# Inverse blocks loaded through POOL's queue instead of SP's, their products six steps later

## The chip, the cores and the metric

The kernel runs on one core of a Trainium2 chip. The metric is the device time of one launch in microseconds (us); lower is better. Five engines work side by side, each through its own instructions in order: PE (matrix products), DVE and ACT (elementwise), POOL (elementwise, and it can issue DMA transfers), SP (issues DMA transfers only). An engine that waits at an instruction holds back everything behind it in its own queue.

## The reference

A two-layer decoder trunk over 512 positions of width 2048. Layer 0 is attention (a sparse group and a latent group). Layer 1, where the change lies, is RWKV-7: six mixed versions of the normed input are projected, and a 64x64 state per head (32 heads) is updated position by position.

```python
def step(state, inp):
    r_t, w_t, k_t, v_t, kk_t, a_t = inp
    sa = jnp.einsum('bhvk,bhk->bhv', state, -kk_t)
    state = (state * w_t[:, :, None, :] + sa[..., None] * (kk_t * a_t)[:, :, None, :]
             + v_t[..., None] * k_t[:, :, None, :])
    return state, jnp.einsum('bhvk,bhk->bhv', state, r_t)
...
xs = tuple(t.transpose(1, 0, 2, 3) for t in (r_h, w_h, k_h, v_h, kk, a_h))
_, y = lax.scan(step, s0, xs)
```

Then each head's output is normed, a bonus is added, a gate is applied, and one more projection leads to the residual and the final norm.

## The kernel before

Matrix products in float32 are done as three passes over split operands (`mm3`, L115 to L118: high by high, low by high, high by low), each of 128 rows by 512 columns. A weight tile of 512 KB (eight such blocks) is fetched by `wload` (L97): one DMA on SP's queue (L103) into one of two raw buffers, then a split by ACT (L85) and DVE (L86) into one of three pairs of split buffers. So PE can run only a few tiles ahead of the last weight that SP has fetched.

**The RWKV layer in chunks.** The 512 positions are cut into 8 chunks of 64, so that the scan becomes products of 64x64 blocks. That needs, for each chunk and head, the inverse of a triangular 64x64 matrix. The 32 heads are 16 pairs p, and four pairs make a group g (4 groups). For pair p, `pair` (L918) builds the operands; its last part (L986 to L994) makes the triangular blocks on PE (tile `pat`, L991), masks them on DVE (L993) and stores them to DRAM (`atd`, L994, on SP's queue).

**The inverses.** Behind the fourth pair of a group (p = 3, 7, 11, 15), three things are put into the program:

- `inverse` (L853): POOL loads the 32x32 diagonal blocks back from `atd` into `U` (four DMAs, L859) and inverts them in place by 30 steps of two small operations (L865, L867).
- `store` (L870): POOL transposes half of it into `T` (L872) and writes `U` and `T` to DRAM as `unu` (L873) and `unt` (L874).
- `inverse2` (L876), a generator of three parts. The first part loads eight blocks from DRAM, all on SP's queue: two from `unt` into `t11` (L884), two off-diagonal ones from `atd` into `t12` (L885) and four from `unu` into `u4` (L887). Here `t11`, `t12` and `u4` have one buffer each. The second part (L889 to L897) makes 64 products of 32x32 blocks of `t12` and `t11` on PE (tile `pv1`) and evicts them by ACT. The third (L899 to L907) makes 64 products with `u4` (tile `pu`), evicts them by DVE and stores the group's whole inverses (`utd`, L907, on SP's queue).

In the trace the tiles `t11` and `t12` have the name `inv2t`, `u4` has the name `u`, and `pv1` the name `pv`.

**What sets the order.** PE's order is written out by hand: `dense` (L1043) is one long stream of steps, a step being the three passes of one 128-row block; `fill(n)` (L1082) runs n steps, and `at(n, f)` (L1079) puts f into the program when n more steps have run. The five parts of `pair` p start around a step t0, which goes up by 18 for the first six pairs and by 22 for the rest; the triangular blocks come at t0 + 32. The three parts of `inverse2` come 70, 98 and 106 steps after the group's fourth pair (L1000). This stage of the kernel ends at step t0 + 32 + 108 of the last pair (L1098), and then the recurrence begins (L1102), which mixes its own small products with the rest of the stream (L1261 on). The other engines' queues are ordered by a scheduler that works from the program's order and its own cost estimates. All of SP's DMAs, weights among them, stand in one queue in that order.

## Time and profile before

| what | value |
|---|---|
| median of 3 runs | 2518.12 us (2512.82 to 2518.66) |
| profiled execution, its own time | 2516.01 us |
| profiled execution, span from first to last instruction | 2514.2 us |
| PE busy, of the span | 2257.8 us (90%) |
| DVE, ACT, POOL busy | 1604.8, 1020.3, 587.4 us |
| mean granted TensorE clock, of full speed | 0.957 |

The span is what the trace shows, from its first instruction to its last; the profiled execution's own time also holds the 1.8 us that lie around it. All stretches named below are in us from the span's start. The stage of the pairs and inverses, with the four groups, lies at about 1230 to 1775, and the recurrence at 1775 to 2320. Busy shares are averages over stages with different limits; what counts for an edit is which wait ends last in its own stage.

### The profile page before, as it was taken

The page shows a single profiled execution, that of the slowest core. Times are in us where ns is not written, and L with a number is a line of the kernel's source. Part 1 is how long each engine was busy: PE and PEld are TensorE (multiplying, and loading weights), DVE is VectorE, ACT ScalarE, POOL GpSimd, SP SyncE. Part 2 cuts the span into 40 slices and gives each one's busy share as a digit, 9 for nine tenths or more (in the row PEclk, how much of TensorE's full clock was granted, in tenths as well). Part 3 has the DMA queues.
Part 4 walks back from the last instruction along what each step waited for, and adds up shares of the span by engine and source line. Part 5 has one row for each costly group of instructions (what it writes and reads, how often), then busy time and mean ns, then how long its engine had stood idle before and what let it go on. Part 6 is the DMA issues. An engine that isn't in the chain of part 4 may idle for free. (4 is left out here: it accounts for less than half of the span.)

```text
span 2514.2 us, 38073 instructions
## 1 busy us (share of the span) xinstructions
PE 2257.8 (90%) x14148; PEld 1749.1 (70%) x14148; DVE 1604.8 (64%) x2983; ACT 1020.3 (41%) x1809; POOL 587.4 (23%) x823
## 2 busy tenths in 40 slices
PE   6789999999989989989995896886899999997997
PEld 3567777777767768866774774665677677775786
DVE  6973677778675557458565574661566666666755
ACT  3343344444454442233764665451133334444222
POOL 1100022222230101100025081643333333320111
PEclk9999999999999999999998897998999999999998
DMA  8973554444222268644674778774656654435864
GB/s 313 325 233 127 171 176 154 156 159 151 72 79 94 76 208 304 216 150 154 204 210 122 233 215 238 213 227 120 178 147 191 214 151 135 133 109 181 307 204 140
DMA packets 256124, 452.03 MB, mean 180 GB/s; under 512 B 104257, under 2 KB 118721, under 8 KB 254657
## 3 DMA queue, kind: packets, MB, share of 16 engines
q1 hardware_dynamic: 239426, 404.49, 50.1%
q0 software_dynamic: 14208, 43.01, 6.5%
q8 instruction: 111, 1.82, 0.3%
q10 hardware_dynamic: 2304, 2.10, 0.2%
q14 instruction: 75, 0.61, 0.1%
HBM read 365.88 MB, written 83.63 MB: 179 GB/s over the span
## 5 line engine op out<-in xcount | busy, mean ns | idle before, releaser
L86 DVE TENSOR_TENSOR wl<-raw,wh 128x1024 fp32r<-128x1024 f32 (+3 forms) x314 | 372.9, 1189 | 225.2 <-ACT wh L85 222.8
L85 ACT ACTIVATE wh<-raw 128x1024 fp32r<-128x1024 f32 (+3 forms) x314 | 313.4, 1000 | 491.7 <-PE pw L118 74.5
L199 DVE CUSTOM_DVE_ANT_0 adaw<-adaw,sc,mod 128x512 f32<-128x512 f32 (+1 forms) x160 | 158.8, 995 | 59.3 <-DMA adaw<-in_ada 57.1
L116 PE MATMUL ps_v<-xh,wh 128*128 128x512 f32 x256 | 109.8, 429 | 68.6 <-ACT wh L85 50.3
L199 DVE CUSTOM_DVE_ANT_0 adaw<-adaw,sc,vec 128x1024 f32<-128x1024 f32 (+1 forms) x96 | 121.1, 1262 | 45.5 <-DMA adaw<-in_ada 45.2
L116 PE MATMUL ps_r<-xh,wh 128*128 128x512 f32 x256 | 109.4, 427 | 19.9 <-ACT wh L85 18.5
L116 PE MATMUL pwo<-xho,wh 128*128 128x512 f32 (+1 forms) x288 | 109.7, 381 | 10.1 <-ACT xho L85 8.7
L470 POOL TENSOR_TENSOR pcmn<-csn,cmn 128x128 f32<-128x128 f32 x48 | 25.6, 560 | 394.3 <-ACT pn L291 206.6
L117 PE MATMUL pwo<-xho,wl 128*128 128x512 f32 (+1 forms) x288 | 108.6, 378 | 4.2 <-DVE wl L86 4.2
L116 PE MATMUL ps_z<-xh,wh 128*128 128x512 f32 x256 | 111.7, 436 | 0.0
L117 PE MATMUL ps_v<-xh,wl 128*128 128x512 f32 x256 | 106.5, 416 | 3.2 <-DVE wl L86 3.2
L118 PE MATMUL pwo<-xlo,wh 128*128 128x512 f32 (+1 forms) x288 | 109.3, 380 | 0.0
L116 PEld LDWEIGHTS ps_v<-xh,wh 128*128 128x128 f32 x256 | 51.3, 200 | 82.7 <-ACT wh L85 52.0
L118 PE MATMUL ps_v<-xl,wh 128*128 128x512 f32 x256 | 105.6, 412 | 0.1
L116 PE MATMUL pw<-yh,wh 128*128 128x512 f32 x256 | 101.5, 397 | 2.9 <-ACT yh L85 2.7
L118 PE MATMUL pw<-yl,wh 128*128 128x512 f32 x256 | 102.1, 403 | 2.0 <-DVE yl L86 2.0
L117 PE MATMUL ps_r<-xh,wl 128*128 128x512 f32 x256 | 102.8, 402 | 0.5 <-DVE wl L86 0.5
L118 PE MATMUL ps_r<-xl,wh 128*128 128x512 f32 x256 | 102.7, 401 | 0.4 <-DVE xl L745 0.4
L117 PE MATMUL pw<-yh,wl 128*128 128x512 f32 x256 | 101.4, 397 | 0.4 <-DVE wl L86 0.4
L118 PE MATMUL ps_z<-xl,wh 128*128 128x512 f32 x256 | 101.8, 397 | 0.0
L117 PE MATMUL ps_z<-xh,wl 128*128 128x512 f32 x256 | 101.6, 397 | 0.0
L499 POOL TENSOR_SCALAR pn<-pn,recn 128x128 f32<-128x128 f32 (+3 forms) x128 | 83.0, 666 | 32.6 <-DVE recn L495 31.1
(463 smaller groups left out, 6206.4 us busy)
## 6 DMA issues: line engine op xcount, KB each, us to landing
adaw<-in_ada SPq DMA_DIRECT2D x128, 512.0 KB, 6.9
adaw<-in_ada SPq DMA_DIRECT2D x128, 256.0 KB, 3.2
raw<-in_win_b SPq DMA_DIRECT2D x58, 512.0 KB, 3.7
raw<-in_rwo SPq DMA_DIRECT2D x36, 512.0 KB, 4.5
raw<-in_wout SPq DMA_DIRECT2D x32, 512.0 KB, 4.5
raw<-in_rwv SPq DMA_DIRECT2D x32, 512.0 KB, 5.4
raw<-in_rwr SPq DMA_DIRECT2D x32, 512.0 KB, 4.5
raw<-in_rwz SPq DMA_DIRECT2D x32, 512.0 KB, 3.9
```

The source lines that it names most:

```text
L85: nc.scalar.activation(hi, src, AF.Copy)
L86: nc.vector.tensor_tensor(lo, src, f32(hi), op=ALU.subtract)
L116: nc.tensor.matmul(ps, ah, bh, start=start, stop=False)
L117: nc.tensor.matmul(ps, al, bh, start=False, stop=False)
L118: nc.tensor.matmul(ps, ah, bl, start=False, stop=stop_)
L199: nc.vector.tensor_tensor_reduce(w, w, self.sc[:, i - self.i0:i - self.i0 + self.n], 0.5, v_("ada_b", layer * 48 + j) if i == 0 else m, op ...
L470: nc.gpsimd.tensor_tensor(pcm[:, :, r], cs, cm[:, 3][:, :, None].to_broadcast([P, 4, 32]), op=ALU.mult)
L499: nc.gpsimd.tensor_scalar(pb[i, b][:, :n], pb[i, b][:, :n], rec[:, i, b:b + 1], 1.0, op0=ALU.mult, op1=ALU.mult)
```

## The change

The eight loads of `inverse2` go from SP's queue to POOL's; the two parts on PE come 104 and 112 steps behind the group's fourth pair instead of 98 and 106; the stage's end is put six steps later to match. No arithmetic is changed, and no transfer is added or dropped.

```diff
             for h in range(2):
                 lo, hi = slice(64 * h, 64 * h + 32), slice(64 * h + 32, 64 * h + 64)
-                nc.sync.dma_start(t11[lo], tv[h])
-                nc.sync.dma_start(t12[lo], blocks(g, h, 0, 1))
+                nc.gpsimd.dma_start(t11[lo], tv[h])
+                nc.gpsimd.dma_start(t12[lo], blocks(g, h, 0, 1))
                 for b in range(2):
-                    nc.sync.dma_start(uu[(lo, hi)[b], :, 32 * b:32 * b + 32], uv[b, h])
+                    nc.gpsimd.dma_start(uu[(lo, hi)[b], :, 32 * b:32 * b + 32], uv[b, h])
...
                 inv = inverse2(p // 4)
-                for n in (70, 98, 106):
+                for n in (70, 104, 112):
                     at(n, lambda: next(inv, None))
...
-        while now[0] < t0 + 32 + 108:
+        while now[0] < t0 + 32 + 114:
             fill(1)
```

How the queues change can be read from the program's order of instructions. The first place is SP's queue around the loads of group 0 (a difference: rows with - stand only in the kernel before, rows with + only in the changed one; `raw` are weight tiles, `hin` inputs of the next version, `kpd` a scratch store):

```order
-L884 DMA inv2t11_0_12125<-unt_9906 32x32x32
+L103 DMA raw578_12190<-in_rwv 128x1024
 L767 DMA hin3_10_11959<-hd_9894 128x512
 L767 DMA hin3_11_11975<-hd_9894 128x512
 L916 DMA kpd_9902<-vf15_12052 128x512
-L887 DMA u4_10686<-unu_9905 32x32x32
+L103 DMA raw579_12254<-in_rwv 128x1024
 L767 DMA hin3_12_11988<-hd_9894 128x512
 L767 DMA hin3_13_12001<-hd_9894 128x512
```

Where the loads of `unt` and `unu` stood among the inputs of the next version, weight tiles stand now; the same holds at the other three groups.

The second place is POOL's queue between groups 0 and 1:

```order
 L873 DMA unu_9905<-U0_11496 128x1024
 L874 DMA unt_9906<-T0_11563 64x1024
+L887 DMA u4_10686<-unu_9905 32x32x32
+L884 DMA inv2t11_0_12125<-unt_9906 32x32x32
+L887 DMA u4_10686<-unu_9905 32x32x32
+L884 DMA inv2t11_0_12125<-unt_9906 32x32x32
+L887 DMA u4_10686<-unu_9905 32x32x32 x2
 L859 DMA U1_12748<-atd_9903 32x32x32 x4
+L885 DMA inv2t12_1_13470<-atd_9903 32x32x32
 L860 MEMSET U1_12748 128x32
 L865 TENSOR_TENSOR Ut1_12754<-U1_12748 128x30
+L885 DMA inv2t12_1_13470<-atd_9903 32x32x32
```

Six loads now follow the two stores, and the two of `t12` stand at the head of each group's inversion, one of them in front of its first operation.

The third place is PE at the first product of the inverses of group 0 (`pat6` are the triangular blocks of pair 6, `ps_v` the value projection):

```order
 L118 MATMUL ps_v1_2_12253<-xl3_15_12026,wh580_12336 128x512
-L991 MATMUL pat6_12461<-kk6_12093,bk6_12226 64x64 x16
+L991 MATMUL pat6_12391<-kk6_12093,bk6_12226 64x64 x16
+L895 MATMUL pv1_00_12411<-inv2t11_0_12125,inv2t12_0_12126 32x32 x32
+L895 MATMUL pv1_01_12446<-inv2t11_0_12125,inv2t12_0_12126 32x32 x32
 L116 MATMUL ps_v1_3_12484<-xh3_0_11765,wh581_12486 128x512
```

The products moved behind the end of one projection tile and behind the triangular blocks of pair 6; before, they stood six blocks earlier in the same tile.

## Rows read from the trace of the kernel before

**Rows 1.** Busy time by stretch: us, busy (count) by engine, PEclk, DMA share, GB/s.

```profile
1293.70:1774.60 480.90, 381.66 (x2871) 301.84 (x2870) 262.65 (x367) 230.07 (x361) 206.73 (x286) 0.89 0.68 198
1411.00:1499.00 88.00, 84.91 (x718) 68.26 (x716) 64.50 (x89) 61.95 (x104) 43.13 (x55) 1.00 0.78 242
1499.00:1550.00 51.00, 26.10 (x133) 20.07 (x135) 19.21 (x26) 17.79 (x30) 10.20 (x14) 0.70 0.63 174
```

**Rows 2.** PE's waits from 1293.7 to 1774.7: us in total, times, longest us.

```profile
PE ps_v L116 <- ACT wh L85: 50.3, 4, 23.8
PE ps_r L116 <- ACT wh L85: 18.5, 1, 18.5
PE ps_v L116 <- ACT xh L744: 18.2, 2, 17.7
```

**Rows 3.** SP's waits in the same stretch (same columns).

```profile
SPq L884 <- DMA unt<-T: 58.4, 4, 25.9
...
SPq L887 <- DMA unu<-U: 24.9, 1, 24.9
```

**Rows 4.** SP's timeline at group 0: start us, us, then engine, line, operation.

```profile
1337.12 0.32 SPq L916 DMA_DIRECT2D kpd<-vf  x1
1363.36 0.33 SPq L884 DMA_DIRECT2D inv2t<-unt  x1
```

**Rows 5.** PE's timeline, one row of each kind and the stage's ends (same columns).

```profile
1293.68 1.15 PE L991 MATMUL pat<-kk,bk 64*64 64x64 f32 x32
...
1338.44 0.40 PE L116 MATMUL ps_v<-xh,wh 128*128 128x512 f32 x1
...
1349.64 0.39 PE L116 MATMUL pl<-lh,l2hrw 96*128 96x512 f32 x1
...
1412.16 2.21 PE L895 MATMUL pv<-inv2t,inv2t 32*32 32x32 f32 x128
...
1418.70 1.15 PE L991 MATMUL pat<-kk,bk 64*64 64x64 f32 x32
...
1441.08 0.66 PE L1020 MATMUL pvt<-ca,vf 128*128 128x128 f32 x4
...
1478.29 1.15 PE L991 MATMUL pat<-kk,bk 64*64 64x64 f32 x32
...
1650.79 1.15 PE L991 MATMUL pat<-kk,bk 64*64 64x64 f32 x32
...
1774.65 0.46 PE L1141 MATMUL g<-kr,bk 64*128 64x128 f32 x2 [1.09 <-DMA kr<-krd]
```

**Rows 6.** POOL's timeline in groups 0 and 3 (same columns).

```profile
1309.20 0.16 POOL L860 MEMSET U<- 128x32 f32 x1 [4.17 <-DMA U<-atd]
...
1358.95 0.61 POOL L873 DMA_DIRECT2D unu<-U  x1
...
1669.95 0.15 POOL L860 MEMSET U<- 128x32 f32 x1 [8.07 <-DMA U<-atd]
...
1716.36 0.61 POOL L873 DMA_DIRECT2D unu<-U  x1
1716.96 0.56 POOL L874 DMA_DIRECT2D unt<-T  x1
```

**Rows 7.** Line 859, POOL's loads of U: issue in ns min/median/max, and landing.

```profile
L859 POOL DMA_DIRECT2D U<-atd x16: 783/786/1017, 1301.7 to 1661.1; - x16
...
DMA to landing us min/median/max: 4.1/5.4/8.7
```

**Rows 8.** Line 874, the store of unt: from issue to landing.

```profile
DMA to landing us min/median/max: 3.7/3.9/4.2
```

**Rows 9.** Line 884, the load from unt on SP's queue: from issue to landing.

```profile
DMA to landing us min/median/max: 2.4/3.7/5.9
```

**Rows 10.** The page's groups: DVE's split of a weight (busy, mean ns of one).

```profile
L86 DVE TENSOR_TENSOR wl<-raw,wh 128x1024 fp32r<-128x1024 f32 (+3 forms) x314 | 372.9, 1189 | 225.2 <-ACT wh L85 222.8
```

**Rows 11.** PE's timeline behind the recurrence.

```profile
2327.48 0.79 PE L116 MATMUL pwo<-xho,wh 128*128 128x512 f32 x1 [8.73 <-ACT xho L85]
```

## The prediction

> **What bounds the kernel now.** I read the busy time by stretch first, because shares over the whole span hide stages. From the triangular blocks of pair 3 (group 0) to the first product of the recurrence, 1293.68 to 1774.65 us [rows 5], the stage takes 481.0 us. PE is busy for 381.66 of 480.90 us there, so it idles 99.2 us, and the granted clock is 0.89 [rows 1]. Between groups it reads otherwise: from 1411 to 1499 PE is busy for 84.91 of 88 us at clock 1.00, from 1499 to 1550 for 26.10 of 51 us at 0.70 [rows 1]. The idle time comes in lumps.
>
> PE's waits say for what: 50.3 and 18.5 us for the split of a weight, 18.2 us for the inputs of the next version, single ones up to 23.8 us [rows 2]. Splits and inputs both start with a DMA on SP's queue, so I asked SP next. SP waits 58.4 us in four waits at L884 for the store of `unt`, and 24.9 us in one at L887 for `unu` [rows 3]: 83.3 us, once per group. The timeline shows the shape: SP issues a store at 1337.12 and nothing until the load of `unt` at 1363.36 [rows 4]. That store comes out of POOL's inversion, whose own store of `unu` leaves at 1358.95 [rows 6]. The weights stand behind the waiting load, and PE runs dry.
>
> **What the change moves.** Thirty-two DMAs (eight per group) leave SP. SP then never waits for POOL's inversion in front of a weight; what is left of it there is `utd`, which waits for PE's own products.
>
> *The stage without the lumps.* Between the two ends PE has 1366 passes of 512 columns, 13 sets of triangular blocks, 16 sets of transposes of `vf`, and four each of the products `pv` and `pu` (counted in its order). From 1338.44 to 1349.64 run 48 passes, 0.2333 us each [rows 5]. The others take 1.15, 0.66 and 2.21 us [rows 5] (`pu` taken as `pv`, its like). So 318.7 + 15.0 + 10.6 + 17.7 = 362.0 us. As a test, pair 6 to pair 9 comes to 60.0 us in this way, and the trace has 59.6 (1418.70 to 1478.29) [rows 5]. The stage's excess is 481.0 - 362.0 = 119.0 us: 99.2 idle, and some 20 of work at the lower of the two clock levels behind each idle time. All of it goes if nothing takes its place.
>
> *The six steps.* They bring 18 passes, 4.2 us, from the recurrence into this stage. The recurrence loses 4.2 us of filler. Behind it PE waits 8.73 us for its result [rows 11], so filler has little value at that end: bounds of the net cost 0 (all given back) and 4.2 us (nothing). I take 4.0, by that row.
>
> *POOL's own cost.* Nearest in shape are the 16 loads of `U`, 0.783 to 1.017 us per issue [rows 7]; I take 0.8. That is 6.4 us per group, beside POOL's other work: it idles more than half of the stage (206.73 of 480.90 us busy) [rows 1], so this costs nothing unless the products on PE come due first. SP in turn gets 32 issues off its queue; it does not bound the stage once it no longer waits, so I count nothing for that.
>
> *When the products come due.* This is what could take the place of the wait. Group 3 is tightest, because no pairs lie behind it: in PE's order, 104 steps (72.8 us), the triangular blocks (1.15), `pv` and `pu` of group 2 (4.4) and two sets of transposes (1.3), so `pv` is due 79.7 us after pair 15's blocks. POOL's side, from 1650.79 [rows 5]: the store of `unu` leaves at 1716.36, 65.6 us on, and that of `unt` 0.6 later [rows 6]. One load of `t12` now lies inside the inversion (0.8); the other is issued while POOL waits for `U` anyway (8.07 us) [rows 6]. So `unt` leaves at 67.0 and lands 3.9 us on [rows 8], at 70.9. Then come L884, L887, L884, the last issued at 72.5. A load lands 3.7 us after issue on SP's queue [rows 9] and 5.4 us for POOL's loads of `U`, 8.7 at worst [rows 7]: 76.2 to 81.2. I take 78, by POOL's own median, and so no wait; at worst 1.5 us. With the products still at 98 steps they would be due at 75.5, so the six steps are what buys the cover.
>
> Group 0 has 84.3 us (72.8, four sets of blocks 4.6, the operand products of three pairs 5.6, two sets of transposes 1.3) and the same path (store at 1358.95, 65.3 us after 1293.68 [rows 5, 6]). Groups 1 and 2 have about 92 us, since four pairs lie between.
>
> *A new wait on POOL.* The first load of `t12` of a group must wait until PE has read the one before. In groups 2 and 3 that product comes 12 to 15 us behind the group's triangular blocks, and POOL waits there with the inversion behind it. With the product (2.2) and the issue (0.8) the inversion is free at 15 to 18 us. In the trace it begins after 15.5 us in group 0 and 19.2 in group 3 (from pat to L860) [rows 5, 6]: group 2 may lose some 3 us of 12 spare ones, group 3 none.
>
> *What the feed can bear.* The stage moves 198 GB/s over 480.90 us; squeezed into about 370 us this is 257, against 242 at a DMA share of 0.78 in the stretch where PE never starved [rows 1]. That stretch idles 3.1 of 88 us, which over the stage would be 13; its idle end already belongs to the next block, so the bounds are 0 and 13, and I take 5.
>
> **The sum.** 2516.0 (the profiled execution's own time) - 119.0 + 5 + 4 + 1 (late products) = 2407 us. This execution lies 2.1 us under the median, so for the median I say 2408 us.
>
> **A page against the rows.** The Trainium skill, "SBUF — State Buffer", section "SBUF: two separate sides", speaks against this move: descriptors of a DMA issued from POOL are written by its own cores, and those are locked out while DVE runs certain copies; it gives 3100 ns instead of 620. By an estimate from that page eight issues per group would end some 20 us later, and the sum would be near 2455. The rows do not bear it out: of 16 issues from POOL the longest took 1.017 us [rows 7], beside a busy DVE.
>
> **The rivals.**
>
> *The products come late.* For it: group 3 has 2 us to spare by my reckoning, group 0 six, and POOL's loads will fly in a denser stage. Against it: the inversion ran in that time beside a fed PE already. If every issue waits for one DVE operation, 1.189 us [rows 10], the path grows by 9.5 us: PE waits 7 to 8 us in group 3 and 3 to 4 in group 0, and with the clock behind it 2408 + 13 = 2421. Twice that delay reaches all groups, some 2455. Chance 0.15; 0.03 of it for the lock at its worst.
>
> *The feed is next.* If transfers or the splits lag, PE idles 5 to 10% of 370 us instead of 5 us: 2421 to 2440. For it: 257 GB/s against 242. Against it: DVE, 64.50 of 88 us busy in the fed stretch [rows 1], has room. Chance 0.12.
>
> *Only issue time is saved.* If SP's wait hid behind something else that stops PE just as long (the inputs, DVE), the gain is SP's issues alone: 32 times 0.8, at most 26 us, and if none lies on PE's path nothing: 2490 to 2518. Against it: the lumps sit at SP's waits, 87 us of them on things that SP fetches [rows 2]. Chance 0.01. The Trainium skill, "DMA: Bandwidth & Descriptors", section "Issuing engines are not separate DMA queues", says as much: more issuing engines save only the time to initiate, usually small. By that rule the time would be the one just given; the rows disagree, since what stands in the queue is a wait and not an issue [rows 3, 4].
>
> *Slower.* POOL's queue now carries a loop: `pv` of one group must end before the next one's load of `t12`, the inversion stands behind that load, and the next `pv` behind the inversion. It decides once the inversion (1309.20 to 1358.95, 49.8 us with the copy [rows 6]) grows so long that the spare times are gone and PE waits more than the 119 us of now in four groups: 30 us each and about 8 to spare, so from 49.8 to 88 us. At twice the length PE would wait some 42 us per group, 168 in all, and at the lower clock behind it 2580. Nothing in the rows comes near; the two inversions shown take 49.8 and 46.4 us. Chance 0.02.
>
> **How the numbers follow.** The forecast has 0.70, the late products 0.15, the feed 0.12, issue time alone 0.01, slower 0.02. The range goes from 2396 (the whole excess gone, the filler free: 2516.0 - 119.0, rounded down) to 2440, which takes in the bounds of the feed (13), of the filler and of the landings, the feed rival and the milder late products; what is left out above and below is about 0.14. A measurement of this kernel tells 0.3% from no change. Faster by more than that: 0.70 + 0.15 + 0.12 = 0.97; within it 0.01; slower 0.02.
>
> **What would show it.** SP's waits at L884 and L887 are gone, and none takes their place beyond the few us at L907. PE is busy for about 97% of the stage at a clock near 1.00, and the stage takes some 370 us. `pv` shows no or a small wait for `inv2t`, in group 3 first. POOL's queue shows a wait before its first load of `t12` in group 2. Behind the recurrence PE waits some 12 us instead of 8.73. I am wrong if PE still has lumps of 10 us or more, wherever they wait, or if POOL's issues take over 1 us.

## The result, and the profile after

The changed kernel takes 2447.02 us (median of 4 runs, 2440.65 to 2447.81) against 2518.1 before in the same comparison: a ratio of 0.9717, 95% interval 0.9696 to 0.9738. Measured once more, with other kernels on another occasion, it took 2439.31 us (2432.07 to 2443.05), ratio 0.9694 (0.9671 to 0.9717). The forecast of 2408 us had the direction and the cause, but it was 39 us too low, and its range, which ended at 2440, stopped 7 us short. That the second measurement lies just inside the range is scatter between the two occasions and no merit of the forecast.

Busy time by stretch of the changed kernel, first the stage between the same two ends as in [rows 1], then two stretches inside it, from the triangular blocks of pair 7 to those of pair 8 and on to those of pair 12 (us, busy and count by engine, PEclk, DMA share, GB/s):

```profile
1297.24:1703.69 406.45, 381.52 (x2889) 303.34 (x2888) 268.60 (x367) 231.38 (x361) 250.34 (x323) 0.96 0.81 237
1414.80:1443.20 28.40, 22.12 (x115) 17.04 (x114) 18.01 (x28) 19.34 (x33) 12.93 (x20) 0.90 0.95 274
1443.20:1527.97 84.77, 80.05 (x574) 63.44 (x573) 60.82 (x80) 58.94 (x98) 55.39 (x70) 0.99 0.88 266
```

The stage went from 481.0 to 406.5 us, with PE idle for 24.9 us instead of 99.2 and a granted clock of 0.96 instead of 0.89. The stage gave 74.5 us back. Ahead of it this execution is 3.6 us longer (1297.24 against 1293.68) and behind it 2.6 (742.1 against 739.5). That makes the 68.4 us between the spans of 2514.2 and 2445.8. In the second measurement's profiled execution the stage is 407.0 us long and begins at 1288.38: the stage repeats well, and what lies ahead of it, where nothing was changed, scatters by some 9 us.

PE's waits from 1290 to 1700 us (total, times, longest), to be read against [rows 2]:

```profile
PE ps_v L116 <- ACT wh L85: 6.2, 2, 4.1
PE ps_v L117 <- DVE wl L86: 5.2, 3, 3.9
PE ps_v L116 <- ACT xh L744: 2.5, 1, 2.5
PE pu L904 <- ACT inv2v L897: 2.3, 1, 2.3
```

The lumps of up to 23.8 us are gone. What is left comes in pieces of some 4 us and less, and no product waits for `inv2t`. SP's waits from 1230 to 1720 us, to be read against [rows 3]:

```profile
SPq L103 <- DVE wl L86: 67.7, 38, 4.2
SPq L960 <- ACT em L959: 37.5, 14, 4.9
SPq L1034 <- DVE epr L1033: 29.0, 6, 11.8
SPq L980 <- DVE bk L979: 25.2, 15, 3.8
```

The 83.3 us at L884 and L887 are gone. The largest waits now are for free weight buffers (L103) and at the pairs' stores (L960, L980, L1034), 11.8 us at the longest. They are not new: in the kernel before, the four lines took 63.6, 34.5, 15.3 and 18.0 us (1230 to 1790). POOL's new lines, each from the view of one line (issue in ns min/median/max; its waits; landing), in the order L884, L885, L887:

```profile
L884 POOL DMA_DIRECT2D inv2t<-unt x8: 783/784/786, 1375.1 to 1671.2; - x8
...
DMA to landing us min/median/max: 4.4/7.5/9.1
...
L885 POOL DMA_DIRECT2D inv2t<-atd x8: 783/795/817, 1308.6 to 1615.9; - x8
...
  PE pv L895: 7.5, 2
...
L887 POOL DMA_DIRECT2D u<-unu x16: 783/783/854, 1372.9 to 1672.7; - x16
...
DMA to landing us min/median/max: 3.3/8.2/10.7
```

An issue costs POOL 0.78 to 0.85 us, as forecast from [rows 7]. But the loads of `unt` land 7.5 us after issue, where it was 3.7 on SP's queue [rows 9], in a stage that moved 198 GB/s instead of 237. The page shows the move as well: SP's queue (`q1`) carries 206146 packets instead of 239426, POOL's (`q0`) 15744 instead of 14208.

### The profile page after: what moved, and what is told of

Its sections match the earlier page's. It is cut to its first block, busy times and chain, and to the rows that moved or that the text cites. A ratio compares the mean times of both kernels' runs of the same rounds, so it can differ in the third digit from the quotient of the medians.

```text
span 2445.8 us, 38074 instructions
## 1 busy us (share of the span) xinstructions
PE 2258.9 (92%) x14148; PEld 1755.3 (72%) x14148; DVE 1609.8 (66%) x2983; ACT 1021.0 (42%) x1809; POOL 628.4 (26%) x855
## 3 DMA queue, kind: packets, MB, share of 16 engines
q1 hardware_dynamic: 206146, 400.30, 51.0%
q0 software_dynamic: 15744, 47.20, 7.6%
## 5 line engine op out<-in xcount | busy, mean ns | idle before, releaser
L116 PE MATMUL pwo<-xho,wh 128*128 128x512 f32 (+1 forms) x288 | 111.2, 386 | 10.7 <-ACT xho L85 7.7
L117 PE MATMUL ps_v<-xh,wl 128*128 128x512 f32 x256 | 104.0, 406 | 5.2 <-DVE wl L86 5.2
L867 POOL TENSOR_TENSOR U<-U,Ut 128x30 f32<-128x30 f32 (+14 forms) x120 | 96.1, 801 | 9.1
L865 POOL TENSOR_TENSOR Ut<-U 128x30 f32<-128x30 f32 (+14 forms) x120 | 91.2, 760 | 9.1
```

The lines of the kernel that those rows point to most:

```text
L116: nc.tensor.matmul(ps, ah, bh, start=start, stop=False)
L117: nc.tensor.matmul(ps, al, bh, start=False, stop=False)
L865: nc.gpsimd.tensor_tensor(tv, U[:, :s_, s_:s_ + 1].to_broadcast([P, s_, n]), U[:, s_:s_ + 1, s_ + 1:].to_broadcast([P, s_, n]), op=ALU.mult)
L867: nc.gpsimd.tensor_tensor(U[:, :s_, s_ + 1:], U[:, :s_, s_ + 1:], tv, op=ALU.add)
```

## Theories after the result

**Theory.** The loss of the kernel before was SP standing at loads whose data was not there yet. What the stage keeps over its priced work (406.5 against 362.0 + 4.2 = 366.2, so 40 us) is the supply of weights: transfers, and loads queued on SP behind stores. **Rivals.** The gain needs POOL's queue as such, or the six steps; the 40 us are ACT's and DVE's own order. Stage lengths below come from one profiled execution each, between the same two ends; the changed kernel gave 406.5 and 407.0 in two of them.

## Experiments: which part of the change did it

**Queue alone.** The loads on POOL, the products and the end where they were:

```diff
-                for n in (70, 104, 112):
+                for n in (70, 98, 106):
...
-        while now[0] < t0 + 32 + 114:
+        while now[0] < t0 + 32 + 108:
```

> The changed kernel with the products back at 98 and 106 steps (stage end at 108), the loads on POOL's queue. Theory (the loss was the wait at the head of SP's queue, and the queue alone removes it): 2440 to 2460 us, with at most a few us of PE waiting for inv2t in group 3, where the changed kernel had about 1 us to spare. Rival (the six steps do a large part): over 2470 us, with PE waits for inv2t of 10 us or more.

Measured: 2444.53 us, ratio 0.9702 (0.9675 to 0.9729). PE's wait for the loads in this kernel:

```profile
PE pv L895 <- DMA inv2t<-unt: 5.7, 2, 3.2
```

The queue alone brings all of the gain that can be measured. The later steps do what the forecast said (without them the products wait twice, 5.7 us), but buy no time that can be measured. The stage is 418.2 us against 406.5, yet the stretch behind it is 735.2 against 742.1.

**Steps alone.** The change with the loads left on SP:

```diff
-                nc.gpsimd.dma_start(t11[lo], tv[h])
-                nc.gpsimd.dma_start(t12[lo], blocks(g, h, 0, 1))
+                nc.sync.dma_start(t11[lo], tv[h])
+                nc.sync.dma_start(t12[lo], blocks(g, h, 0, 1))
...
-                    nc.gpsimd.dma_start(uu[(lo, hi)[b], :, 32 * b:32 * b + 32], uv[b, h])
+                    nc.sync.dma_start(uu[(lo, hi)[b], :, 32 * b:32 * b + 32], uv[b, h])
```

> The kernel before with the products at 104 and 112 steps (stage end at 114), the loads on SP's queue. Theory: SP still waits over 70 us at L884 and L887, and the time stays within 10 us of before, 2508 to 2528. Rival (the six steps do a large part): under 2490.

Measured: 2528.72 us, ratio 1.0053 (1.0036 to 1.0069), the stage 499.7 us. The time is 0.7 us above the theory's range, and SP waits 69.4 us at L884 and 25.4 at L887, a little more than before. By themselves the steps cost time.

**Loads later on SP.** As the run before, with the loads put into the program 98 steps behind the pair, not 70:

```diff
-                for n in (70, 104, 112):
+                for n in (98, 104, 112):
```

> As the last one, but the loads are put into the program 98 steps behind the group's fourth pair instead of 70, still on SP's queue. If the place in the program decides where they stand in SP's queue, the inversion is done by then and SP waits no more: 2435 to 2470. If the scheduler puts them as early as its own estimate allows, as the program's order suggests for group 0, SP's waits remain in part: 2480 to 2520. I expect the second.

Measured: 2559.43 us, ratio 1.0167 (1.0145 to 1.0188), slower than either case. PE's and SP's largest waits:

```profile
PE pv L895 <- DMA inv2t<-unt: 79.0, 3, 43.7
```

```profile
SPq L884 <- DMA unt<-T: 88.7, 3, 36.1
```

SP still reaches the loads before the inversion is done, and now the products stand directly behind them. So the later place in the program didn't help here.

**SP without the wait, first try.** The kernel before, its loads reading `atd` instead of `unu` and `unt` (so the inverses are left out), with `T` in the buffer of `v1` (otherwise `T` has the one buffer of `t11`, so that a load of `t11` would still wait for `T`'s store):

```diff
-            T = kw.tile([64, 32, 32], F32, tag="t11", name=f"T{g}", bufs=1)
+            T = kw.tile([64, 32, 32], F32, tag="v1", name=f"T{g}", bufs=1)
...
-                nc.sync.dma_start(t11[lo], tv[h])
+                nc.sync.dma_start(t11[lo], blocks(g, h, 0, 1))
...
-                    nc.sync.dma_start(uu[(lo, hi)[b], :, 32 * b:32 * b + 32], uv[b, h])
+                    nc.sync.dma_start(uu[(lo, hi)[b], :, 32 * b:32 * b + 32], blocks(g, h, b, b))
```

> The kernel before with the loads of t11 and u4 taken from atd instead of unt and unu, still on SP's queue, and T in the buffer of v1, so that no load waits for the inversion (this leaves out the inverses: the values are others). Theory (it is the wait, not the queue or the transfers): 2435 to 2460, as the changed kernel or a little better. Rival (what the change left, some 40 us of the stage over its work, is the loads' doing on POOL's queue, where they land in 8 us instead of 4): under 2430, and PE's waits in the stage fall by half against the changed kernel.

Measured: 2529.11 us, ratio 1.0054 (1.0037 to 1.0071). The shared buffer made a new wait: ACT's eviction into `v1` had to wait until `T` was stored (62.5 us in two waits), and PE's `pu` waited 92.5 us for it, 47.4 at once. The run says nothing on the queue.

**SP without the wait, second try.** The same reads, with `T`, its copy and its store left out:

```diff
-            T = kw.tile([64, 32, 32], F32, tag="t11", name=f"T{g}", bufs=1)
-            nc.gpsimd.tensor_copy(T, U[:64].rearrange("p s t -> p t s"))
...
-            nc.gpsimd.dma_start(unt[g], T.rearrange("p s t -> p (s t)"))
```

> The kernel before with all its loads still on SP, but reading tensors that the inversion doesn't write: t11 and the two blocks of u4 come from atd, as t12 does, and T with its copy and its store is left out (so the output isn't the reference's). No load of SP then waits for the inversion, and no buffer is shared that could make a new wait, as v1's did in the run before. Theory (the whole loss of the kernel before was SP standing at loads whose data was not yet there, and the queue as such is no matter): 2430 to 2455 us, the SP waits on unt and unu gone (109 us before), PE's waits on wh at ps_v down from 50 us to under 15. Rival (a good part of the gain is that SP has 32 fewer instructions and transfers of short runs, whatever they wait for): 2470 to 2500.

Measured: 2457.05 us, ratio 0.9782 (0.9763 to 0.9802), the stage 423.8 us. With all 32 loads still on SP, taking away what they wait for brings 2.2% of the change's 2.8 to 3.1%. It came out 2 us above the theory's range and 13 below the rival's. (The expectation's 109 us of waits on `unt` and `unu` are the 83.3 of [rows 3].) PE's largest wait in this kernel:

```profile
PE ps_v L116 <- ACT wh L85: 31.7, 4, 12.9
```

The longest of the four, 12.9 us, ends at 1491.16. Ahead of it SP's timeline has 31 us without a weight, between the loads at 1453.74 and 1484.86; in them SP issues stores, inputs and eight of the 32 loads, which take 6.1 us. So the wait was the main part of the loss, and the loads' place in SP's queue, as this example suggests, a smaller one. (The run also spares POOL the copy and the store of `T`.)

**Only `t12` on SP.** The changed kernel, two of each group's eight loads back on SP:

```diff
-                nc.gpsimd.dma_start(t12[lo], blocks(g, h, 0, 1))
+                nc.sync.dma_start(t12[lo], blocks(g, h, 0, 1))
```

> The changed kernel with only the t12 loads (two of each group's eight, whose data has long been there) back on SP. Theory (a load on SP costs only by what it waits for, and POOL's queue lands these short runs in 7.5 us against 3.7 on SP): 2438 to 2450, no difference of note; SP waits for nothing at them but t12's readers. Rival (the six loads and their place in SP's order delay weights, whatever they wait for): over 2455.

Measured: 2461.94 us, ratio 0.9799 (0.9782 to 0.9815), the stage 416.0. The expectation's rival calls the loads on SP six; it is two per group. They wait for nothing there, land in 5.1 us, and the kernel is still 15 us slower or more: the time is the rival's, and it fits the rest that the run before left. In the trace the longer stage comes from one place, between the blocks of pairs 10 and 11 (1480.20 to 1511.94, 31.7 us instead of 18.9), where weights land 10.6 us after issue beside group 1's six loads on POOL. How two issues on SP at 1462.95 and 1473.39 could bring that about isn't shown, nor whether it would come again in another execution.

## Experiments: where the other 40 us went

**Stores off SP.** The stores of a pair that wait for ACT or DVE go to ACT's queue; first all of them (`bkd`, `krd` and `xzd` in the same way), then only those whose data ACT itself wrote (`epd`, `vfd`, `vtd`):

```diff
-            nc.sync.dma_start(epd[p].rearrange("p (c t) -> p c t", t=C), ep[:, :, 1:])
+            nc.scalar.dma_start(epd[p].rearrange("p (c t) -> p c t", t=C), ep[:, :, 1:])
...
-            nc.sync.dma_start(vfd[p], vf)
+            nc.scalar.dma_start(vfd[p], vf)
...
-                    nc.sync.dma_start(vv[a], vt[64 * a:64 * a + 64].rearrange("p (b f) -> p b f", f=P))
+                    nc.scalar.dma_start(vv[a], vt[64 * a:64 * a + 64].rearrange("p (b f) -> p b f", f=P))
```

> The changed kernel with the stores of a pair that wait for ACT or DVE (epd, bkd, both halves of krd, vfd, vtd, xzd) issued by ACT instead of SP. Theory (the stage's residual comes from SP standing at such stores while the next weight tile's load is queued behind them: the longest SP waits left are on em, epr, bk, vt): the gaps of some 20 us between two weight loads go, PE's waits at ps_v fall below 5 us in all, 2415 to 2435. Rival (ACT's order is the limit as well: some 100 issues and its waits on DVE move into the engine that makes wh): 2445 to 2500, with PE's waits on wh above the 6.2 us of the changed kernel.

> The changed kernel with only those stores moved to ACT whose data ACT itself has just written (epd, vfd, vtd), so that ACT waits for nobody new. Theory (SP's standing at em and vt, 53 us of its waits between 1230 and 1720, delays weight loads): half of the gain of moving all stores, 2425 to 2440. Rival (what SP waits for is on time for the weights anyway, the splits on ACT and DVE come late through their own order): 2440 to 2460.

Measured: 2502.05 us, ratio 0.9961 (0.9947 to 0.9975), for all, 2 us above the rival's range; 2457.22 us, ratio 0.9786 (0.9763 to 0.9809), for ACT's own, within the rival's. PE's waits for splits with all of them moved:

```profile
PE ps_v L116 <- ACT wh L85: 20.4, 5, 7.2
PE ps_v L117 <- DVE wl L86: 17.9, 9, 6.4
```

SP no longer stands at those stores, but ACT and DVE get later (38.3 us of waits for their splits, where the changed kernel has 11.4), and SP waits for them elsewhere: 94.6 us for free weight buffers (L103) and 69.0 at the load of `kp` (L931), from 1290 to 1700. What the stores cost on SP these two runs can't tell, since both put their issues into ACT, whose splits PE waits for.

**A third raw weight buffer.** It finds room because `v1` moves into partitions that `t12` leaves free; in the changed kernel, and in the one with the queue alone:

```diff
-        raw = wraw.tile([P, 1024], F32, tag="raw", name=f"raw{u}")
+        raw = (extra[0] if extra and u % 3 == 0 else wraw).tile([P, 1024], F32, tag="raw", name=f"raw{u}")
...
+        extra.append(kp.enter_context(pool(name="wrawx", bufs=1)))
...
-            t11, t12, v1 = (kw.tile([P, 32, 32], F32, tag=n, name=f"inv2{n}_{g}", bufs=1) for n in ("t11", "t12", "v1"))
+            t11, t12 = (kw.tile([P, 32, 32], F32, tag=n, name=f"inv2{n}_{g}", bufs=1) for n in ("t11", "t12"))
+            v1 = t12
```

> The changed kernel with a third buffer for the raw weight tiles while the pairs run (its room comes from the second products' v1, which moves into the partitions of t12 that t12 leaves free). A weight load then waits for the split of three tiles before, not of two, so SP can stand some 7 us longer at a store before the splits lack a tile. Theory (the some 25 us that stay without the loads are stalls of PE where a weight load was queued behind stores on SP): the stage falls from 406 to 380 to 395 us, the kernel to 2422 to 2436. Rival (the splits come late because ACT and DVE are in other work, not because the tile isn't there): 2440 to 2452, no change.

> The same third buffer in the kernel with the queue changed alone (products after 98 and 106 steps). Theory: as the run before, 2420 to 2436; the products' wait for t11 (5.7 us without the later steps) stays. Rival: no change from the queue alone, 2438 to 2450.

Measured: 2435.65 us, ratio 0.9695 (0.9680 to 0.9711), and 2435.38 us, 0.9691 (0.9656 to 0.9727). That looked like a gain, so it was run beside the changed kernel itself:

> The changed kernel once more, unaltered, on the same chip and in the same rounds as the next one, for a direct comparison: 2440 to 2452.

> The changed kernel with the third raw buffer once more. If its 11 us are real: 2430 to 2440, its interval below that of the changed kernel in the same rounds; if they were the chip's: within 5 us of it.

Measured there: the changed kernel 2439.31 us, 0.9694 (0.9671 to 0.9717); with the third buffer 2441.28 us, 0.9694 (0.9672 to 0.9716). There is no gain in the total. The 11 us were the scatter between occasions, and the stages agree: 402.9 and 406.3 us with it, 406.5 and 407.0 without. (With the queue alone the stage went from 418.2 to 404.2 us, one execution each; the totals can't be told apart.)

The traces show where a gain goes. With the third buffer PE has no wait for `wh` left in the stage, but longer ones for ACT's other results; the longest, for `vf`, is 10.4 us at the same place in both of its executions. ACT stands there at inputs that land late, beside group 2's loads on POOL. First PE's wait, a row of ACT's timeline, and how long inputs took to land from 1578 to 1598 (10.0 us in the second execution). Then the landing from 1566 to 1586 in the kernel with the third buffer and without loads (next experiment), where the like wait is 2.0 us:

```profile
PE ps_r L116 <- ACT vf L1016: 10.4, 1, 10.4
...
1588.88 0.72 ACT L742 ACTIVATE mx<-hin,omu 128x512 f32<-128x512 f32 x1 [4.91 <-DMA hin<-hd]
...
hin<-hd SPq DMA_DIRECT2D x4, 256.0 KB, 9.8
```

```profile
hin<-hd SPq DMA_DIRECT2D x7, 256.0 KB, 4.0
```

**No loads at all.** The changed kernel without the eight loads per group; the products read `u4`'s buffer, the inversion and its stores stay. Then the same with the third buffer:

```diff
-            for h in range(2):
-                lo, hi = slice(64 * h, 64 * h + 32), slice(64 * h + 32, 64 * h + 64)
-                nc.gpsimd.dma_start(t11[lo], tv[h])
-                nc.gpsimd.dma_start(t12[lo], blocks(g, h, 0, 1))
-                for b in range(2):
-                    nc.gpsimd.dma_start(uu[(lo, hi)[b], :, 32 * b:32 * b + 32], uv[b, h])
...
-                        nc.tensor.matmul(pv1[hi, c], t12[lo, 16 * q + c], t11[lo, 16 * q + c], start=True, stop=True)
+                        nc.tensor.matmul(pv1[hi, c], uu[lo, 16 * q + c, :32], uu[lo, 16 * q + c, :32], start=True, stop=True)
```

> The changed kernel without the eight loads per group, on any queue: the first products read u4's own buffer in place of t11 and t12, the inversion and its stores remain (the output isn't the reference's). It takes away the loads' 32 issues on POOL and their transfers. Theory (the 40 us that the stage keeps over its priced work come from SP's in-order queue and from the order of ACT and DVE, not from the loads): within 12 us of the changed kernel, 2435 to 2455, the stage between the fourth pat and the first g product at 398 to 410 us. Rival (the loads' transfers of short runs slow the weights' arrival): under 2430, the stage under 390.

> The third buffer together with the loads left out (the output isn't the reference's). If the two causes (the loads' transfers, 15 us of the stage; weight loads queued on SP behind stores, 25 us) are separate and are all there is, the stage comes down to the priced 365 to 378 us and the kernel to 2400 to 2414. Rival (ACT and DVE hold the splits back): 2420 to 2430, as without the third buffer.

Measured: 2427.01 us, ratio 0.9661 (0.9639 to 0.9683), and with the third buffer 2419.34 us, 0.9630 (0.9610 to 0.9649). The stages by stretch, first of the one, then of the other:

```profile
1291.38:1683.04 391.66, 373.56 (x2889) 297.62 (x2889) 269.30 (x367) 231.28 (x361) 220.69 (x289) 0.98 0.75 234
```

```profile
1292.50:1673.51 381.01, 371.37 (x2889) 297.19 (x2889) 267.58 (x367) 231.22 (x361) 225.52 (x289) 0.99 0.78 239
```

The first time is the rival's (its stage, under 390, was missed by 2 us); the second lies between the two ranges, the stage 3 us above the theory's. The loads, off SP's queue and never waited for by PE, still cost the stage 15 us. This run takes away their transfers together with their issues and waits on POOL; that it is the transfers is read from the DMA view. Here is the changed kernel from 1372 to 1388 us, while group 0's six loads are under way (queues: packets, MB, share of 16 engines; issues: KB each, median us to landing), then its weights from 1440 to 1490, with no such loads:

```profile
q1 hardware_dynamic: 1907, 2.58, 66.9%
q0 software_dynamic: 394, 1.09, 31.5%
...
raw<-in_rwv SPq DMA_DIRECT2D x2, 512.0 KB, 12.7
u<-unu POOLq DMA_DIRECT2D x4, 128.0 KB, 9.4
...
raw<-in_rwv SPq DMA_DIRECT2D x7, 512.0 KB, 4.9
```

And the kernel without the loads, from 1372 to 1388:

```profile
q1 hardware_dynamic: 3433, 3.69, 71.8%
...
raw<-in_rwv SPq DMA_DIRECT2D x1, 512.0 KB, 4.7
```

The two queues fill the 16 DMA engines between them (66.9 + 31.5%), and a weight then lands 12.7 us after its issue instead of 4.7. The next groups show 10.8 and 8.0 us in the same place. The Trainium skill, "DMA: Bandwidth & Descriptors", section "Issuing engines are not separate DMA queues", says that transfers from whichever engine run on the same 16 DMA engines and interleave; the trace agrees. The same section expects little from issuing on more engines; there the 2.8 to 3.1% measured here decide, since what the move saved was a wait.

**Long runs.** The six loads of `unu` and `unt` as whole rows of 4 KB per partition instead of 32 pieces of 128 bytes (the same bytes, in the wrong order):

```diff
-                nc.gpsimd.dma_start(t11[lo], tv[h])
+                nc.gpsimd.dma_start(t11[lo].rearrange("p s t -> p (s t)"), unt[g, 32 * h:32 * h + 32])
...
-                    nc.gpsimd.dma_start(uu[(lo, hi)[b], :, 32 * b:32 * b + 32], uv[b, h])
+                    nc.gpsimd.dma_start(uu[(lo, hi)[b], 16 * b:16 * b + 16].rearrange("p c t -> p (c t)"), unu[g, 64 * b + 32 * h:64 * b + 32 * h + 32])
```

> The changed kernel with the six loads of unu and unt in long runs: each partition fetches one whole row of 4 KB instead of 32 pieces of 128 bytes, the same bytes from the same tensors into the same tiles on the same queue, behind the same waits (the blocks arrive in the wrong order, so the output isn't the reference's). Theory (the loads cost the stage 15 us because their short pieces fill the DMA engines, three times, beside the weights: in the changed kernel raw lands in 12.7, 10.8 and 8.0 us there, in 4 to 5 outside): raw lands in under 7 us in these places, the stage falls from 406 to 388 to 396 us, the kernel to 2426 to 2436. Rival (bytes, POOL's issues or the waits for the inversion cost it, not the pieces): 2442 to 2450, raw still at 8 to 12 us.

Measured: 2435.86 us, ratio 0.9686 (0.9666 to 0.9706), beside 0.9694 for the changed kernel on the same occasion: no difference that can be told. The stage is 400.3 against 407.0 us. Weights land in 10.0, 9.4 and 6.2 us beside the loads, against 10.7, 10.4 and 8.6. So the shortness of the pieces is at most a part, by the landing times the lesser one; the theory's under 7 us came true in one place of three.

**Half the weights' bytes.** While the pairs run, only the first half of each weight tile is fetched and split twice (the second half of each tile's values is left out); in the changed kernel, and in the one before:

```diff
+        if halfs and n == 1024:
+            t2 = lambda t: t.rearrange("p (a b) -> p a b", a=2)
+            nc.sync.dma_start(raw[:, :512], src[:, :512])
+            r2_ = raw[:, None, :512].to_broadcast([P, 2, 512])
+            nc.scalar.activation(t2(hi), r2_, AF.Copy)
+            nc.vector.tensor_tensor(t2(lo), r2_, t2(f32(hi)), op=ALU.subtract)
```

> The changed kernel fetching, while the pairs run, only the first half of each weight tile (256 KB in place of 512 KB); the splits read that half twice, so every split, matmul, wait and issue stays and only the bytes go (the output isn't the reference's). Some 50 tiles of the stage, 13 MB of its 96 MB. Theory (what is left of the stage's excess is the DMA engines: 329 us of their time are to go through a stage that would otherwise be 366 us): the share of DMA in the stage falls from 0.81 under 0.75, the stage from 406 to 370 to 385 us, the kernel to 2400 to 2420. Rival (SP's order and the order of ACT and DVE set the splits, whatever the bytes): stage over 398, kernel over 2434.

> The same halved weight loads in the kernel before, where the loads stand on SP. Theory (there SP stands 83 us at loads whose data isn't ready, and bytes are not short): 2495 to 2520, the SP waits on unt and unu still over 70 us. Rival (bytes are the bound in both kernels): under 2480.

Measured: 2430.60 us, ratio 0.9669 (0.9637 to 0.9700), and 2508.39 us, 0.9990 (0.9976 to 1.0003). The stages, first in the changed kernel, then in the one before, and the latter's waits on SP:

```profile
1295.15:1686.75 391.60, 376.43 (x2890) 300.93 (x2889) 267.56 (x367) 230.04 (x361) 252.05 (x321) 0.97 0.74 212
```

```profile
1288.10:1764.57 476.47, 377.61 (x2871) 299.93 (x2871) 258.72 (x367) 230.84 (x361) 203.18 (x285) 0.89 0.61 173
```

```profile
SPq L895 <- DMA unu<-U: 52.9, 2, 27.9
SPq L892 <- DMA unt<-T: 47.5, 3, 24.1
```

In the kernel before, 13 MB fewer change nothing: SP stands at the loads (L892 and L895 here) for 100 us all the same. In the changed kernel they bring 15 us of the stage, as much as leaving out the loads; in the total the interval still overlaps that of the changed kernel's second measurement. Bytes cost time only once the wait was gone. But the stage stopped at 391.6, between the two cases: bytes are one part of the 40 us, not all.

**More traffic.** The changed kernel with four extra copies per group on POOL's queue, from memory to memory:

```diff
+            for i in range(4):
+                nc.gpsimd.dma_start(more[g, i], d["rwv"][4 * g + i][:, :512])
```

> The changed kernel with four copies from tensor to tensor in memory (256 KB each) issued by POOL behind each group's eight loads: 4 MB more, nothing waits for them. Theory (DMA engines full): each burst beside the weights lasts longer, the stage 8 to 25 us longer, the kernel 2450 to 2470. Rival (bytes are not what is short): within 5 us of the changed kernel, 2436 to 2450.

Measured: 2459.82 us, ratio 0.9792 (0.9770 to 0.9814), which looks like the theory's case and isn't. The view of the new tensor:

```profile
L890 POOL DMA_DIRECT2D more<-in_rwv x16: 523/523/725, 1.3 to 17.4; - x16
```

The copies depend on nothing, so the scheduler put all sixteen at the very start (1.3 to 17.4 us). The stage is 408.9 us, as without them; it merely begins later, at 1309.14. The run says nothing on the stage.

## Why the prediction was right and where it failed

**Right: the bound and the direction.** SP's 83.3 us of waits were what PE's lumps came from. Take the wait away and the lumps go (on POOL or, for the most part, on SP); take bytes away and they stay. The rival that only issue time is saved fell, and so did the slower one.

**Right: POOL's price and its cover.** Issues take 0.78 to 0.85 us as forecast. The wait before the first load of `t12` appears where it was forecast: two waits for `pv`, 7.5 us in all, and no product came late for it. The inversion of group 0 did stretch, from 49.8 us to 57.0 (1312.65 to 1369.65): 0.8 us is the load inside it, the rest its own small operations, of which some took longer at the same shape (the last of 128x130 1.47 us instead of 0.45); why isn't shown. The loads' landing was taken as 5.4 us and is 7.5 to 8.2, but the products still didn't wait, and at the old steps they wait 5.7 us. The Trainium skill, "SBUF — State Buffer", section "SBUF: two separate sides", has 3100 ns instead of 620 for a DMA from POOL whose descriptors have to wait. No issue here shows such a wait: the longest of 32 took 854 ns. Whether any of the longer landing comes from it no run tells.

**About right: the filler.** The six steps were forecast to cost 4 us that the recurrence doesn't pay back. The stretch behind the stage took 742.1 and 740.8 us against 739.5, so none came back; in the total, where the queue alone takes as long, the 4 us can't be seen. What was to show it didn't: PE waits 7.72 us for the result behind the recurrence, not 12.

**Failed: "what the feed can bear".** This term stood at 5 us with bounds 0 and 13. It measured 40 (406.5 less 366.2): 24.9 us of PE idle and some 15 of work at the lower clock level; the second execution has 27.9 and 13. That is most of the miss: of the 41 us by which the profiled execution exceeds the sum (2407), 34 lie in the stage (406.5 against 362.0 + 4.2 + 5 + 1), 3.6 ahead of it, where nothing was changed, and some 3 behind it. (The step from 2407 to 2408 is a slip: with the 2.1 us named there it is 2409.) The prediction's own signs of being wrong, waits of 10 us or more and issues over 1 us, did not show: it watched for long waits, and the loss came in short ones. PE is busy for 94% of the stage at a clock of 0.96, not 97% near 1.00. Three things were wrong in the term.

- *The witness was a better stretch than the stage would be.* The 88 us from which the bound came moved 242 GB/s at a DMA share of 0.78 [rows 1]. The squeezed stage wanted 257. Its DMA work (0.68 of 481.0 us before, 0.81 of 406.5 after: 327 and 329 us) would have filled 0.90 of 366 us, and the witness showed nothing of how PE fares at 0.90. The share alone doesn't decide it, though: from pair 7 to pair 8 the changed kernel idles 6.3 of 28.4 us at 0.95, and with the third buffer PE runs through the same work without a gap at 0.98 (last row of the fence of stretches below).
- *The moved loads themselves were priced as issues, not as transfers.* Before, SP's own wait kept weights out of their way. On POOL's queue they fly beside the weights; in three groups, with the DMA engines full, weights then land late. Without the loads the stage is 15 us shorter.
- *Small stalls were priced without the clock behind them.* The prediction added that price to the lumps and to late products, but not here. PE's timeline of the changed kernel shows one stall (the pass before it, the first two and the last of 13 slow passes, then two at the upper level):

```profile
1369.59 0.39 PE L116 MATMUL ps_v<-xh,wh 128*128 128x512 f32 x1
1373.85 0.79 PE L117 MATMUL ps_v<-xh,wl 128*128 128x512 f32 x1 [3.87 <-DVE wl L86]
1374.44 0.63 PE L118 MATMUL ps_v<-xl,wh 128*128 128x512 f32 x1
...
1379.13 0.49 PE L117 MATMUL ps_v<-xh,wl 128*128 128x512 f32 x1
1379.46 0.40 PE L118 MATMUL ps_v<-xl,wh 128*128 128x512 f32 x1
1379.70 0.40 PE L116 MATMUL ps_v<-xh,wh 128*128 128x512 f32 x1
```

and by stretch:

```profile
1373.85:1380.00 6.15, 6.15 (x16) 4.86 (x17) 3.13 (x7) 0.63 (x1) 3.88 (x5) 0.55 0.92 263
```

The granted clock is 0.55 there, mostly the lower of its two levels (1.2 and 2.4 GHz). From 1373.85 to 1379.46 run 13 passes, 0.43 us each, where 13 take 3.03 us at the upper level: the stall of 3.87 us costs 2.6 more. Over the stage the ratio is much the same (15 behind 25, and 13 behind 28). In the long lumps of the kernel before it was 20 behind 99.

**The rival that came nearest** is "the feed is next". Its idle share of 5 to 10% was right (24.9 of 406.5 us is 6%), but it too left the clock out, and so ended at 2440, where 2447 came. With 1.6 us for each us of idle time (24.9 idle, 40 in all) it runs from 2433 to 2462: 2403 us without the feed's term, and 18.5 to 37 us of idle.

**What stays open.** Of the 40 us, some 15 go with the loads, and some 15 with half the weights' bytes. Both weren't tried together, but the traces tell where each lies: the changed kernel from the blocks of pair 15 to the stage's end, then pair 7 to pair 8 and pair 15 to the end without the loads, the same two with half the bytes, and pair 7 to pair 8 with the third buffer:

```profile
1589.83:1703.69 113.86, 110.00 (x943) 88.44 (x942) 49.55 (x68) 37.69 (x50) 65.44 (x97) 0.94 0.77 203
...
1405.40:1434.57 29.17, 22.39 (x116) 17.14 (x115) 18.43 (x28) 19.03 (x32) 11.37 (x19) 0.88 0.83 259
1578.99:1683.04 104.05, 103.68 (x943) 83.89 (x943) 50.59 (x68) 36.01 (x49) 57.80 (x85) 0.99 0.69 202
...
1414.39:1433.74 19.35, 19.35 (x115) 15.62 (x115) 13.55 (x22) 14.73 (x25) 5.50 (x9) 1.00 0.90 247
1575.05:1686.75 111.70, 107.56 (x944) 86.57 (x943) 50.40 (x70) 36.79 (x49) 70.78 (x102) 0.95 0.72 182
...
1411.70:1431.05 19.35, 19.35 (x116) 15.62 (x115) 12.50 (x21) 14.21 (x25) 6.20 (x10) 1.00 0.98 284
```

Leaving out the loads shortens the stretch at the end, which begins while group 2's loads are under way, from 113.9 us to 104.0 and leaves the other at 29; half the bytes take that one from 28.5 to 19.4 us and the one at the end only to 111.7. (The changed kernel's second execution has 113.7 and 29.7.) So, by one execution of each, the two are for the most part not the same 15 us. The third buffer, too, takes pair 7 to pair 8 to 19.4 us; with the loads there the stage loses this again, some 2 to 4 us at each of four other places, one of them with the 10.4 us wait shown above. Without them the third buffer took the stage 11 us further, to 381.0. At pair 7 to pair 8, SP's timeline has 18 us between two weight loads, in which SP stops at stores and inputs (first and last row, and one of the stops), and PE's longest wait, 4.1 us for `wh`, follows at 1436.98:

```profile
1409.13 1.02 SPq L103 DMA_DIRECT2D raw<-in_rwv  x1
...
1422.69 0.53 SPq L983 DMA_DIRECT2D krd<-kk  x1
...
1427.33 0.42 SPq L103 DMA_DIRECT2D raw<-in_rwv  x1
```

Some 15 us are left even without the loads and with the third buffer (381.0 less 366.2). That they come from the order of SP, ACT and DVE is likely but not shown: no experiment made them go. No version that leaves nothing out beats the changed kernel: with the queue alone, with a third buffer or with both, it can't be told from it.

## What to carry to other kernels

In an engine's queue of transfers, look for a load whose data another engine still has to make: everything behind it waits too, and moving it to the engine that makes the data removed that wait here without an earlier result. Price the moved transfers twice, as issues on the new queue and as traffic that now flies beside what used to be held back. And when a big idle time goes, price the small ones that stay with the clock behind them: here each us of idle cost 1.5 to 1.6, where the long lumps before had cost 1.2.

## What the runs showed that was not expected

- The same 32 loads count 1040 packets each on SP's queue (239426 less 206146, by 32) and 48 on POOL's (15744 less 14208, by 32), and yet those of `unt` land later there, 7.5 us instead of 3.7. In the dense stage alone the difference is smaller: the loads of `t12` land in 6.4 us from POOL's queue and in 5.1 from SP's.
- Whole rows of 4 KB instead of pieces of 128 bytes took the issue on POOL from 0.78 to 0.49 us, but the landing hardly (medians 7.0 for both tensors, against 6.7 and 8.0).
- A change of place in the program's text need not move a transfer: sixteen copies written behind the pairs ran in the first 17 us.
